# Values of nine of twelve heads turned to tokens by transposing DMA transfers

## The chip, the core and the metric

One core of a Trainium2 chip runs the whole program. Its engines work at the same time, each through its own queue in order: TensorE (PE, with its weight loads PEld), VectorE (DVE), ScalarE (ACT), GpSimd (POOL) and SyncE (SP). SP's queue issues the DMA transfers of the kernel before, and 16 DMA engines carry them out. Waits between engines are semaphores. The metric is the time of one execution on the device in microseconds; lower is better.

## The reference

A trunk of two layers on 528 tokens (16 learned meta tokens ahead of 512 given ones), each of 1024 numbers. Each layer normalises the rows, projects them, mixes the tokens, multiplies with a SiLU gate and projects back. The first is gated linear attention with 4 heads:

```python
S_new = exp(b_last) * S + einsum('bhjd,bhjv->bhdv', k * exp(b_last - b), v)
o = einsum('bhij,bhjv->bhiv', attn, v) + einsum('bhid,bhdv->bhiv', q * exp(b), S)
```

The second is differential attention with 8 heads, the difference of two softmaxes with a shared position bias:

```python
p = softmax(s, axis=-1)
a = p[:, :, 0] - lam * p[:, :, 1]
o = einsum('bhqk,bhkv->bhqv', a, vh)
```

In both, the values v stand on the contracted side: the product over tokens needs them with tokens on the partitions. A head of the first layer has 512 value columns, one of the second 256.

## The kernel before

All matrix products run as three products of rounded parts: a number is split into a high part (fp32r) and a low part, its rest. `split` (line 237) has ACT write the high part (line 240) and DVE the low part (line 241). `split3` (line 328) does the same for 32 short rows that carry the 16 meta tokens, with the parts below each other in one tile (lines 333, 334, 338).

In the projections the weights are the stationary operand, so each result comes out turned: columns of the projection on the partitions, 528 tokens along the row. Most of them are done by halves with seven products in place of eight: a `Unit` (line 362) computes four pieces of a 2 x 2 block product, with sums of weights that DVE makes beforehand (line 296) and partial results that ACT copies out of PSUM (`partial`, line 378). A product is 12 matmuls into one of the banks bx, by and bv. When a piece of 128 columns is complete, the unit calls its `tail(i)`, with i = 1 and then 0.

The weights come by DMA on SP's queue into two buffers named raw (lines 249 and 256). A buffer is free for the next load when DVE's last split has read it.

`Weaver` (line 73) weaves two streams of work into PE's order, which is written out by hand: the attention's own steps, and a queue of projections as generators. `fill(us)` runs that much of the queue, `finish` runs it to a stop mark, and every yielded amount of PE time goes through `spent`, which counts down the steps deferred by `defer`. The order on ACT, DVE, POOL and SP is left to a scheduler; what is marked `urgent` moves forward by 100 places in it.

The values arrive as two pieces a unit. For the first layer, `q_gla_v` (line 755) makes two units a head, so four pieces; each tail calls `turned_back` (line 758), which defers by 2.4 us of PE time a `post`: `to_tokens` (line 730) transposes the piece on PE, four blocks of 128 x 128 (line 735) and one of 128 x 32 for the short rows (line 736), into two PSUM tiles, and `split` and `split3` take them from there into s.v and s.vm. For the second layer `q_diff_v` makes one unit a head, and `turned_back2` (line 1381) does the same with tokens in reversed order. Head 0 of either layer goes its own way (`plain_unit`, and a projection at the layers' boundary), but through the same two functions. This makes 16 + 16 pieces.

`gla_blocks` uses a first-layer head's values when the queue of its projections is finished. In the second layer the step C (`values`, line 1497) uses them, after A (`scores`), B (`turn`: the attention matrix transposed on PE and split into aT and am) and before E (`rows`). For the four blocks b the written order is A3 A2 B3 A1 C3 B2 E3 A0 C2 B1 E2 C1 B0 E1 C0 E0, so B of the next block always stands behind C of the last one.

`b_all` (line 482) holds the first layer's decay sums, one row of 528 for each of 8 column tiles. hT, yt and the others are the residual and intermediate tiles.

Of the kernel before, what the change touches and what calls it, by code (L numbers as in the profile page):

```python
# [11 lines left out]
F32 = mybir.dt.float32  # L12
F32R = mybir.dt.float32r
I32 = mybir.dt.int32
AF = mybir.ActivationFunctionType
ALU = mybir.AluOpType
AX = mybir.AxisListType
# [2 lines left out]
P = 128  # L20
D = 1024
NM = 16
M3 = 96
NR = 512
# [48 lines left out]
class Weaver:  # L73


    def __init__(self):
        self.queue, self.late, self.left, self.stop = deque(), [], 0.0, None

    def add(self, gen, us=0.0):
        self.queue.append(gen)  # L80
# [7 lines left out]
    def defer(self, us, fn):  # L88
        self.late.append([us, fn])

    def spent(self, us):
        for d in self.late:
            d[0] -= us
        while self.late and self.late[0][0] <= 0:
            self.late.pop(0)[1]()
# [33 lines left out]
class Weights:  # L129
# [44 lines left out]
    def done(self, p):  # L174
        self.room[p.kind] += 1
        self.pump()
# [8 lines left out]
def trunk(ctx, tc, x, meta, g_norm, gla_w_in, gla_w_gate_up, gla_b_gate, gla_gnorm, gla_w_out,  # L185
# [3 lines left out]
    act, dve, pe, pool, sp = nc.scalar, nc.vector, nc.tensor, nc.gpsimd, nc.sync  # L189
# [17 lines left out]
    def T(p, shape, dt, tag, **kw):  # L207
        uid[0] += 1
        return p.tile(shape, dt, tag=tag, name=f"{tag}_{uid[0]}", **kw)
# [62 lines left out]
    W = Weaver()  # L272
# [208 lines left out]
    X = {n: x_parts(i) for i, n in enumerate(("b11", "b21", "b22", "t1", "t2", "t4"))}  # L481
    b_all = T(kp, [P, KT, L], F32, "keep")
    hp = ctx.enter_context(tc.tile_pool(name="hp", bufs=1))
    gctx = ctx.enter_context(ExitStack())
    hT = T(hp, [P, KT, L], F32, "hT")
    gp = gctx.enter_context(tc.tile_pool(name="gp", bufs=1))
# [3 lines left out]
    def tmp():  # L490
        return T(tp, [P, L], F32, "t")


    ones = cp.tile([P, P], F32, name="ones")
    dve.memset(ones, 1.0)
# [18 lines left out]
    for b in range(5):  # L514
        t0, n = BLK[b]
# [239 lines left out]
    def q_gla_v(hd, s):  # L755
        us = [want_unit(g_w_in, 2048 + 512 * hd + c) for c in (0, 256)] if hd else v_first

        def turned_back(m, vt):
            def post():
                pt, pm = to_tokens(vt, BLK, vt[:, :32])  # L760
                cs = slice(m * P, (m + 1) * P)
                split(s.v[0][:, :, cs], s.v[1][:, :, cs], pt.rearrange("p (b c) -> p b c", b=4))
                split3(s.vm[:, cs], pm, 32, short[:, NM:NM + 1])
            W.defer(2.4, post)

        gens = []
        for h, u in enumerate(us):
            vts = []

            def dst(h=h, vts=vts):  # L770
                if h == 0:
                    s.vm = T(gp, [M3, 512], F32R, "vm0")
                    s.v = [T(gp, [P, 4, 512], F32R, f"v{i}") for i in range(2)]
                vts.extend([tmp(), tmp()])
                return vts

            if hd:
                gens.append(W.add(Unit(u, X, 1.0, dst, lambda i, h=h, vts=vts: turned_back(2 * h + i, vts[i]))))
            else:
                def evac(i, banks, h=h, vts=vts, dst=dst):  # L780
                    if i == 0:
                        dst()
                    for n, bank in enumerate(banks):
                        act.activation(vts[i][:, n * HT:(n + 1) * HT], bank[:, :HT], AF.Copy)
                    turned_back(2 * h + i, vts[i])

                gens.append(W.add(plain_unit(u, evac)))
        return gens[0]
# [356 lines left out]
    for hd in range(G_HEADS):  # L1145
        s = heads[hd]
        last = hd == G_HEADS - 1
        if hd:
            if not last:
                q_gla_out(hd - 1, heads[hd - 1])  # L1150
            for half in range(2):
                q_gla_z(hd, s, half)
            if not last:
                W.stop = q_gla_qk(hd + 1, heads[hd + 1])[0]
            if hd == 1:
                second_layer_setup()
            W.fill(4.0)
        if hd == 0:
            W.fill(2.0)
        gla_scores(hd, s)  # L1160
        W.fill(5.0)
        gla_ready(hd, s)
        if hd == 0:
            hot = T(gp, [P, TLEN], F32, "kd")
            sp.dma_start(hot[:NBUCK + 1], c_hot)
        W.finish()
        W.settle()
        if hd == 0:
            for m in range(4):
                gla_gate(0, s, m, h2(s.z[:, m, :]))  # L1170
        if hd == 0:
            q_gla_qk(1, heads[1])
        W.stop = None
        if last:
            q_gla_out(hd - 1, heads[hd - 1])
        else:
            W.stop = q_gla_v(hd + 1, heads[hd + 1])
        gla_blocks(hd, s, (1.2, 1.2) if last else (1.9, 1.6), last)
        W.finish()
        W.stop = None  # L1180
# [200 lines left out]
    def turned_back2(s, m, vt, first=False):  # L1381
        if not first:

            urgent(dve.tensor_copy)(vt[:, HT:HT + 8], vt[:, 2 * HT:2 * HT + 8])

        @urgent
        def post():
            end = L if first else 272
            pt, pm = to_tokens(vt, RBLK if first else HBLK, vt[:, end - 32:end])
            cs = slice(m * P, (m + 1) * P)  # L1390
            split3(s.vm[:, cs], pm, 32, short[:, NM + 1:NM + 2])
            split(s.v[0][:, :, cs], s.v[1][:, :, cs], pt.rearrange("p (b c) -> p b c", b=4))
        W.defer(2.2 if s is not heads[-1] else 1.4, post)

    def q_diff_z(hd, s):
        zts = []
# [59 lines left out]
    def diff_steps(hd, s, ys):  # L1456
# [26 lines left out]
        @urgent  # L1483
        def turn(r):
            b, a = r.b, r.p[0]
            pt, pm = ps_tile(), ps_tile()
            for j in range(b + 1):
                pe.transpose(pt[:, j * P:(j + 1) * P], a[:, j * P:(j + 1) * P], ident)  # L1488
            pe.transpose(pm[:32, :P], a[:, r.nk - 32:r.nk], ident)
            r.am = T(ep, [M3, P], F32R, "am")  # L1490
            r.aT = [T(ep, [P, 512], F32R, f"aT{i}") for i in range(2)]
            w = (b + 1) * P
            split(r.aT[0][:, :w], r.aT[1][:, :w], pt[:, :w])
            split3(r.am, pm[:32, :P], 64)
# [129 lines left out]
    for hd in range(D_HEADS):  # L1624
        last = hd == D_HEADS - 1
        s = heads[hd]
        W.finish(projs[hd])
        W.settle()
        s.scored = False
        out2 = None  # L1630
        keep = {D_HEADS - 1: 0.0, D_HEADS - 2: 22.0}.get(hd, 3.0)
        if hd in (2, 4, 6):
            out2 = q_diff_out2(hd - 2, ys[hd - 2:hd])
        if not last:
            n = heads[hd + 1]
            late = hd == D_HEADS - 2
            if not late:
                gates.append(q_diff_z(hd + 1, n))
                values.append(q_diff_v(hd + 1, n))
            W.stop = q_diff_k(hd + 1, n)  # L1640
            projs.append(q_diff_q(hd + 1, n))
            if late:
                values.append(q_diff_v(hd + 1, n))
                gates.append(q_diff_z(hd + 1, n))
        if hd == D_HEADS - 2:
            ws.room["none"] = 0
            wt = want_last(hd)

            def freed():
                ws.room["none"] += 2  # L1650
                ws.pump()
            gates[-1].freed = freed
        (A, B, C, E), o = diff_steps(hd, s, ys), (3, 2, 1, 0)
        steps = [(A, 0), (A, 1), (B, 0), (A, 2), (C, 0), (B, 1), (E, 0), (A, 3), (C, 1), (B, 2), (E, 1), (C, 2), (B, 3),
                 (E, 2), (C, 3), (E, 3)]
        steps = [(f, o[i]) for f, i in steps]
        share = {A: 1.5, B: 1.1, C: 1.1, E: 0.5}
        if last:
            steps = steps[:6]
        W.fill(3.0)  # L1660
        for n, (f, b) in enumerate(steps):
            if last and n == 4:
                if values[hd] in W.queue:
                    W.finish(values[hd])
                W.settle()
                W.fill(2.0)
            if n == 5 and gates[hd] in W.queue:
                W.finish(gates[hd])
            if last and n == 5:
                gfin = T(xp, [P, D], F32, "x0", bufs=1)  # L1670
                sp.dma_start(gfin, g_final.partition_broadcast(P))
            if n == 5:
                if out2 in W.queue:
                    W.finish(out2)
                ys.append([yt[:, hd % 2, i] for i in range(2)])
            f(b)
            if f is A and b == 0:
                s.scored, W.stop = True, None
                if not last:
                    heads[hd + 1].T = bias_tile(hd + 1)  # L1680
            W.fill(max((W.left - keep) * share[f] / sum(share[g] for g, _ in steps[n:]),
                       (4.0 if hd % 2 == 0 else 3.0) if n == len(steps) - 2 else 2.4 if f is C else 0.0))
# [56 lines left out]
```

## Time and profile before

| | |
|---|---|
| median of 3 runs | 996.02 us (995.7 to 997.62) |
| the profiled execution | 998.37 us, its span 996.6 us |
| instructions in the span | 18277 |
| DMA | 84.24 MB, mean 85 GB/s |
| granted TensorE clock, mean | 0.994 |

A row of the groups' view names line, engine, operation, written tile <- read tiles, shapes and count, then the busy time in us and the mean of one in ns, then the idle time of the engine just before them and what ended it. A row of the timeline has its start and its length in us, the engine, the line, the operation and how many were merged; in brackets stands the idle time before it and the releaser. In the table of stretches there follow on the stretch its length, the busy time and count of PE, PEld, DVE, ACT and POOL, the granted clock, DMA's busy share and GB/s. The view of waits names who waited for whom: total us, times, longest. An issue row of DMA gives count, KB of each and the median time from issue to landing. Weight loads and matmuls overlap; some matmul records are missing (120 of 128 on line 735).

### The profile page before, as it was taken

The page shows a single profiled execution, that of the slowest core. Times are in us where ns is not written, and L with a number is a line of the kernel's source. Part 1 is how long each engine was busy: PE and PEld are TensorE (multiplying, and loading weights), DVE is VectorE, ACT ScalarE, POOL GpSimd, SP SyncE. Part 2 cuts the span into 40 slices and gives each one's busy share as a digit, 9 for nine tenths or more (in the row PEclk, how much of TensorE's full clock was granted, in tenths as well). Part 3 has the DMA queues.
Part 4 walks back from the last instruction along what each step waited for, and adds up shares of the span by engine and source line. Part 5 has one row for each costly group of instructions (what it writes and reads, how often), then busy time and mean ns, then how long its engine had stood idle before and what let it go on. Part 6 is the DMA issues. An engine that isn't in the chain of part 4 may idle for free. (4 is left out here: it accounts for less than half of the span.)

```text
span 996.6 us, 18277 instructions
## 1 busy us (share of the span) xinstructions
PE 979.5 (98%) x7143; PEld 925.1 (93%) x7143; DVE 783.2 (79%) x1586; ACT 596.7 (60%) x1304; POOL 48.3 (5%) x68
## 2 busy tenths in 40 slices
PE   8999999999999999999999999999999999999997
PEld 7999999999999999999899898899998999988896
DVE  7888886878777788565998886888967878767785
ACT  7675854365535656536667676366764666645584
POOL 1000000001000100000000100000010010000001
PEclk8999999999999999999999999999999999999999
DMA  7213322132233312222332322333322332323212
GB/s 194 79 50 85 88 84 84 49 108 61 85 85 85 85 47 82 86 85 85 96 86 69 88 68 96 85 97 85 85 96 81 82 103 56 110 62 93 85 65 85
DMA packets 121161, 84.24 MB, mean 85 GB/s; under 512 B 6365, under 2 KB 110077, under 8 KB 121072
## 3 DMA queue, kind: packets, MB, share of 16 engines
q1 hardware_dynamic: 121072, 83.05, 28.8%
q8 instruction: 56, 0.92, 0.4%
q14 instruction: 33, 0.27, 0.1%
HBM read 83.64 MB, written 2.12 MB: 86 GB/s over the span
## 5 line engine op out<-in xcount | busy, mean ns | idle before, releaser
L240 ACT ACTIVATE wh<-raw 128x1024 fp32r<-128x1024 f32 x99 | 104.4, 1055 | 59.6 <-PE by L830 26.9
L241 DVE TENSOR_TENSOR wl<-raw,wh 128x1024 fp32r<-128x1024 f32 x99 | 120.9, 1221 | 24.3 <-ACT wh L240 16.3
L357 PE MATMUL bv<-x,wh 128*128 128x264 f32 (+1 forms) x656 | 97.3, 287 | 0.0
L357 PE MATMUL bx<-x,wh 128*128 128x264 f32 (+1 forms) x640 | 95.2, 286 | 1.0 <-ACT u L378 1.0
L357 PEld LDWEIGHTS bv<-x,wh 128*128 128x128 f32 x656 | 86.3, 189 | 0.3
L357 PEld LDWEIGHTS bx<-x,wh 128*128 128x128 f32 x640 | 84.6, 188 | 2.0 <-ACT u L378 1.5
L241 DVE TENSOR_TENSOR wl<-sum,wh 128x1024 fp32r<-128x1024 f32 x41 | 50.1, 1222 | 21.7 <-ACT wh L240 19.6
L378 ACT ACTIVATE u<-bx 128x264 f32<-128x264 f32 (+1 forms) x120 | 45.4, 379 | 32.4 <-PE bx L357 30.4
L347 PE MATMUL bx<-x,wh 128*128 128x512 f32 (+1 forms) x256 | 62.4, 385 | 0.0
L1475 ACT ACTIVATE p<-p,st 128x528 f32<-128x528 f32 (+3 forms) x64 | 36.4, 569 | 39.2 <-DVE st L1473 39.2
L357 PE MATMUL bv<-x,wl 128*128 128x264 f32 (+1 forms) x328 | 56.4, 286 | 0.0
L357 PE MATMUL bx<-x,wl 128*128 128x264 f32 (+1 forms) x320 | 54.6, 285 | 0.0
L240 ACT ACTIVATE wh<-sum 128x1024 fp32r<-128x1024 f32 x41 | 43.3, 1055 | 18.2 <-PE by L830 9.6
L347 PEld LDWEIGHTS bx<-x,wh 128*128 128x128 f32 x256 | 44.5, 188 | 7.9
L1511 POOL TENSOR_TENSOR st<-st,mhalf 128x1 f32<-128x1 f32 x32 | 28.1, 879 | 474.3 <-ACT on L1509 426.3
L357 PE MATMUL by<-x,a12h 128*128 128x264 f32 (+1 forms) x320 | 46.5, 285 | 0.0
L357 PEld LDWEIGHTS bv<-x,wl 128*128 128x128 f32 x328 | 46.2, 189 | 0.1
L357 PE MATMUL bx<-x,a11h 128*128 128x264 f32 (+1 forms) x320 | 46.2, 285 | 0.0
L240 ACT ACTIVATE a11h<-raw 128x512 fp32r<-128x512 f32 x41 | 25.8, 628 | 33.2 <-DMA raw<-in_diff_w_in_dram 17.6
L357 PEld LDWEIGHTS bx<-x,wl 128*128 128x128 f32 x320 | 45.3, 188 | 0.1
L357 PEld LDWEIGHTS bx<-x,a11h 128*128 128x128 f32 x320 | 42.3, 189 | 0.8
L357 PEld LDWEIGHTS by<-x,a12h 128*128 128x128 f32 x320 | 41.7, 188 | 0.0
(465 smaller groups left out, 2652.4 us busy)
## 6 DMA issues: line engine op xcount, KB each, us to landing
raw<-in_gla_w_in_dram SPq DMA_DIRECT2D x48, 512.0 KB, 4.2
raw<-in_diff_w_in_dram SPq DMA_DIRECT2D x42, 512.0 KB, 5.6
raw<-in_diff_w_in_dram SPq DMA_DIRECT2D x11, 1024.0 KB, 5.8
raw<-in_gla_w_out_dram SPq DMA_DIRECT2D x8, 1024.0 KB
raw<-in_diff_w_out_dram SPq DMA_DIRECT2D x8, 1024.0 KB, 5.0
T<-bdr SPq DMA_DIRECT2D x8, 264.0 KB
out_dram<-x SPq DMA_DIRECT2D x8, 256.0 KB, 2.1
kd<-steep SPq DMA_DIRECT2D x4, 400.0 KB
```

The costliest lines, as they stand in the source:

```text
L240: act.activation(hi, src, AF.Copy)
L241: dve.tensor_tensor(lo, src, hi.bitcast(F32), op=ALU.subtract)
L347: pe.matmul(bank, a[:, k, :], b[k] if n0 is None else b[k][:, n0 + i * nn:n0 + (i + 1) * nn], start=n == 0 and ks[0] == 0, stop=n == len(t ...
L357: pe.matmul(bank[:, :x[q].shape[2]], w[p][:, k * P:(k + 1) * P], x[q][:, k, :], start=first and i == 0, stop=i == len(PASSES) - 1, skip_gr ...
L378: act.activation(t, self.bx[:, :self.n], AF.Copy, scale=self.sc)
L1475: act.activation(p[:, :nk], p[:, :nk], AF.Exp, scale=-1.0, bias=st[:, m:m + 1], accum_out=st[:, 2 + m:3 + m])
L1511: pool.tensor_tensor(ms, ms, mhalf[:, :1], op=ALU.pow)
```

## The change

For heads 1 to 3 of the first layer and heads 1 to 6 of the second, `to_tokens` is no longer called. In its place `turn_by_dma` handles a pair of pieces:

- `leave(m, src)`, called by a unit's tail: ACT copies the piece into a plane, as 16-bit words, all low halves of the 32-bit numbers first and all high halves behind them; ACT then issues a DMA that writes the plane to DRAM (vd, three buffers).
- When both pieces have left, `follow` puts two steps on the weaver's list: `turn` after 6.0 us of PE time, and `done` another 9.0 us later.
- `turn`: SP issues transposing DMAs of 16-bit words from vd back into the planes' own bytes (one of four blocks in the first layer, two of two blocks in the second, where the slices reverse the order of the blocks), and one more for the short rows into a tile `lands`. Rows of vd are ordered piece, partition, half; so the two halves of a number land next to each other, and both pieces of the pair side by side.
- `done`: `split` and `split3` read from the landed tiles, once for the pair, 256 columns wide.

The planes of the first layer lie in rows of b_all whose decays have been read; those of the second are a new tile with one buffer. For its room aT and am have one buffer where they had two. `land` empties the list: before a head's `gla_blocks`, and at the start of a head of the second layer.

```diff
 class Weaver:
+        self.away = []
...
+    def follow(self, *steps):
+        self.away.append([steps[0][0], list(steps)])
+
+    def onward(self, us=0.0):
+        for d in list(self.away):
+            d[0] -= us
+            while d[0] <= 0:
+                d[1].pop(0)[1]()
+                if not d[1]:
+                    self.away.remove(d)
+                    break
+                d[0] += d[1][0][0]
+
+    def land(self):
+        while self.away:
+            self.onward(1000.0)
+
     def spent(self, us):
+        self.onward(us)
...
+    def words(t):
+        return t.bitcast(U16)
+
+    def turn_by_dma(planes, groups, ends, done):
+        n = planes.shape[2]
+        vd = T(dp, [2, P, 2, n], U16, "vd", bufs=3)
+        rows = vd.rearrange("m p h c -> (m p h) c")
+        raw = planes.rearrange("p m c -> p (m c)")[:, :2 * NR].rearrange("p (b c) -> p b c", c=2 * P)
+        left, lands = [0, 1], []
+
+        @urgent
+        def leave(m, src):
+            pl = words(planes[:, m, :]).rearrange("p (h c) -> p h c", h=2)
+            act.activation(pl, words(src).rearrange("p (c h) -> p h c", h=2), AF.Copy)
+            act.dma_start(vd[m], pl)
+            left.remove(m)
+            if not left:
+                W.follow((6.0, turn), (9.0, lambda: done(raw, lands[0][:32, 0, :])))
+
+        def turn():
+            for blocks, c0 in groups:
+                o = words(raw[:, blocks, :])
+                sp.dma_start(o, rows[:, c0:c0 + P * o.shape[1]], transpose=True)
+            lands.append(T(mp, [P, 1, 2 * P], F32, "lands"))
+            sp.dma_start(words(lands[0]), rows[:, ends:ends + P], transpose=True)
+
+        return leave
...
+        def turner(h):
+            @urgent
+            def done(pt, pm):
+                cs = slice(256 * h, 256 * h + 256)
+                split(s.v[0][:, :, cs], s.v[1][:, :, cs], pt)
+                split3(s.vm[:, cs], pm, 32, short[:, NM:NM + 1])
+            return turn_by_dma(b_all[:, 2 * h:2 * h + 2, :], [(slice(0, 4), NM)], 0, done)
...
-                gens.append(W.add(Unit(u, X, 1.0, dst, lambda i, h=h, vts=vts: turned_back(2 * h + i, vts[i]))))
+                gens.append(W.add(Unit(u, X, 1.0, dst, lambda i, vts=vts, leave=turner(h): leave(i, vts[i]))))
...
+        W.land()
         gla_blocks(hd, s, (1.2, 1.2) if last else (1.9, 1.6), last)
...
-        W.defer(2.2 if s is not heads[-1] else 1.4, post)
+        @urgent
+        def done(pt, pm):
+            split3(s.vm, pm, 32, short[:, NM + 1:NM + 2])
+            split(s.v[0], s.v[1], pt)
+
+        if first or s is heads[-1]:
+            W.defer(2.2 if first else 1.4, post)
+        else:
+            if m:
+                s.leave = turn_by_dma(T(ep, [P, 2, 536], F32, "planes", bufs=1),
+                                      [(slice(3, 1, -1), 0), (slice(1, None, -1), 272)], 240, done)
+            s.leave(m, vt[:, :536])
...
-            r.am = T(ep, [M3, P], F32R, "am")
-            r.aT = [T(ep, [P, 512], F32R, f"aT{i}") for i in range(2)]
+            r.am = T(ep, [M3, P], F32R, "am", bufs=1)
+            r.aT = [T(ep, [P, 512], F32R, f"aT{i}", bufs=1) for i in range(2)]
...
         W.settle()
+        W.land()
         s.scored = False
```

More of the change, by code (lines that the diff above doesn't have):

```diff
@@ L14 @@
 I32 = mybir.dt.int32
+U16 = mybir.dt.uint16
 AF = mybir.ActivationFunctionType
@@ L483, in trunk @@
     hp = ctx.enter_context(tc.tile_pool(name="hp", bufs=1))
+    mp = ctx.enter_context(tc.tile_pool(name="mp", bufs=1))
     gctx = ctx.enter_context(ExitStack())
```

## The prediction

> **What bounds the kernel now.** I read the page's first part, then the stretches of the span, then PE's own view around one of the groups that the change removes.
>
> ```profile
> span 996.6 us, 18277 instructions
> ...
> PE 979.5 (98%) x7143; PEld 925.1 (93%) x7143; DVE 783.2 (79%) x1586; ACT 596.7 (60%) x1304; POOL 48.3 (5%) x68
> ...
> PEclk8999999999999999999999999999999999999999
> ...
> q1 hardware_dynamic: 121072, 83.05, 28.8%
> ```
> ```profile
> 146.00:250.00 104.00, 103.52 (x817) 100.12 (x816) 79.81 (x152) 54.71 (x107) 3.57 (x5) 1.00 0.29 82
> 250.00:355.00 105.00, 104.69 (x833) 102.37 (x833) 81.97 (x153) 57.31 (x111) 3.57 (x5) 1.00 0.28 81
> ...
> 530.00:910.00 380.00, 379.32 (x2607) 351.26 (x2606) 299.19 (x653) 231.09 (x556) 23.37 (x25) 1.00 0.29 85
> ```
>
> The columns of the second fence are stretch, length, then PE, PEld, DVE, ACT and POOL busy, the granted clock and DMA's share. The stretches hold two heads of the first layer and the second layer's heads. PE is idle for 0.3 to 0.7 us in each, at full clock; ACT has 40% to 47% of them free and DVE some 22%. So every slot that leaves PE shortens the span, as long as no other engine makes PE wait; and there is almost no waiting on PE now that could absorb a new one. DMA has 70% of its time free.
>
> **PE: what is removed.** Each of 24 calls of to_tokens loses four transposes of 128x128 and one of 32 columns (lines 735 and 736).
>
> ```profile
> 726.59 0.47 PEld L735 LDWEIGHTS ps<-ident,t 128*128 128x128 f32 x4
> ...
> 727.02 0.10 PEld L736 LDWEIGHTS ps<-ident,t 128*32 128x32 f32 x1
> ...
> 727.13 0.42 PEld L357 LDWEIGHTS bx<-x,wl 128*128 128x128 f32 x3
> ...
> 729.17 1.32 PE L326 MATMUL ps<-v,aT 128*128 128x256 f32 x9
> ```
> ```profile
> L735 PE MATMUL ps<-ident,t x120: 270/272/282, 38.2 to 953.8; 128*128 128x128 f32 x120
> ```
>
> The first weight load of the group starts at 726.59, the first of the product behind it at 727.13: a group holds PE for 0.54 us. 24 x 0.54 = **13.0 us off PE**. A rival that they stay does not arise: in the order of the built program the 120 transposes of tiles t are 24. The Trainium skill, "TensorE: Matmul & The Clock Gate", Part 4, gives about 275 ns for a 128x128 transpose within a kernel. The last row agrees as to the duration (272 ns), but they overlap on PE; five times 275 ns would make an estimate of 33 us for 24 groups, and the starts say 13.0.
>
> **ACT and DVE: what is added and taken away.** For each pair of pieces (12 of them), ACT makes two plane copies of 128x1056 or 128x1072 words (line 532 of the changed kernel), issues two DMAs, and then splits one 128x1024 tile where it split two of 128x512.
>
> ```profile
> L240 ACT ACTIVATE wh<-raw 128x1024 fp32r<-128x1024 f32 x99 | 104.4, 1055 | 59.6 <-PE by L830 26.9 <-PE bv L357 11.1 <-PE bx L347 9.7
> ...
> L240 ACT ACTIVATE v<-ps 128x512 fp32r<-128x512 f32 x32 | 19.0, 595 | 5.9 <-PE ps L735 5.4
> ...
> L334 ACT ACTIVATE vm<-ps,short 32x128 fp32r<-32x128 f32 x32 | 11.3, 357 | 0.5
> ...
> L333 ACT ACTIVATE vm<-ps,short 32x128 fp32r<-32x128 f32 x32 | 10.9, 343 | 0.0
> ```
> ```profile
> 598.05 0.37 SPq L249 DMA_DIRECT2D raw<-in_diff_w_out_dram  x1
> ```
>
> A plane copy by the elements of the 1024-wide row: 1.055 x 1056/1024 = 1.09 us. A DMA's issue by SP's: 0.37. Added: 2 x (1.09 + 0.37) = 2.9 us a pair. Taken away: two splits of 0.595 for one of 1.055 (0.1), and four short ones of 0.34 to 0.36 for two of twice the width, some 0.4 each (0.6). Net 2.2 us a pair, 26 us over 12: ACT goes from 597 to 623 us, still under two thirds. DVE only gets less. As totals both lie beside PE. What counts is the bunch: ACT reads each partial product (line 378) out of bank bx before PE may go on in it, and PE has one product in another bank meanwhile:
>
> ```profile
> 937.02 1.14 PE L357 MATMUL by<-x,a12h 128*128 128x264 f32 x8
> ...
> 938.48 1.14 PE L357 MATMUL bx<-x,wh 128*128 128x264 f32 x8
> ```
>
> One product is 938.48 - 937.02 = 1.46 us, so a bunch on ACT beyond about 1.5 us reaches PE. In the built order both copies and both issues stand back to back in 4 of the 12 pairs, and in a fifth with one weight split between; I count 5: 5 x (2.9 - 1.46) = 7.2; in the other 7 other work stands between, which I price at nothing because 1.46 us of product covers each half. Bounds: 0 (all hidden) to 12 x 1.44 = 17. I take **+7**.
>
> **The new wait.** ACT's split of the landed values waits for a chain: second DMA out, SP's wake-up, transpose in. What stands behind it on ACT are the partial products, the weight splits and the scores' exponentials, and behind those PE. How much time the order leaves for the chain is read from the trace of before at the same neighbours. The first pair's second issue stands behind the copy u of the first row below, and its split behind the cm of the second row; the last pair's between the third and fourth.
>
> ```profile
> 158.25 0.39 ACT L378 ACTIVATE u<-bx 128x264 f32<-128x264 f32 x1 [0.87 <-PE bx L357]
> ...
> 166.41 0.27 ACT L334 ACTIVATE cm<-ps 32x128 fp32r<-32x128 f32 x1
> ```
> ```profile
> 856.61 0.36 ACT L378 ACTIVATE u<-bx 128x264 f32<-128x264 f32 x1
> ...
> 862.13 0.27 ACT L334 ACTIVATE am<-ps 32x128 fp32r<-32x128 f32 x1
> ```
>
> From end to end that is 8.0 us and 5.4 us. Taken so for the 12 pairs (2.9 us off where the bunch stands inside) it lies between 4.7 and 8.4, 6.9 on average. The chain:
>
> ```profile
> raw<-in_gla_w_in_dram SPq DMA_DIRECT2D x48, 512.0 KB, 4.2
> raw<-in_diff_w_in_dram SPq DMA_DIRECT2D x42, 512.0 KB, 5.6
> ...
> out_dram<-x SPq DMA_DIRECT2D x8, 256.0 KB, 2.1
> ```
>
> - Out: 264 to 268 KB like the output's 256 KB, 2.1 us; the second, right behind the first or beside a weight load, at most twice that. I take 3.0.
> - SP: one issue, 0.4.
> - In: 512 KB are transposed, and 128 KB more for the short rows. No row shows a transposing DMA. The nearest is a weight piece of 512 KB: 4.2 us from issue to landing. The short rows add between nothing and a quarter of that (1.05); I take 0.7, since they run on behind the first. Together 4.9.
>
> Sum 8.3, against 6.9: 1.4 us for each pair, on an ACT whose wait goes straight on to PE because the splits behind it come at once. 12 x 1.4 = **+17**. Bounds from the rows: with the transfer at 2.1 us, the fastest of its size class, the chain is 2.1 + 0.4 + 2.1 = 4.6 and nothing is left to wait for: 0, and less than no wait there is not. From above, each partition receives 16-bit words of many rows; the built transfer moves blocks of 16 rows, thus pieces of 32 bytes, 16384 of them for 512 KB. What a tiny piece costs shows where single words were loaded:
>
> ```profile
> DMA packets 1689, 0.01 MB, mean 5 GB/s; under 512 B 1689, under 2 KB 1689, under 8 KB 1689
> ...
> q1 hardware_dynamic: 1689, 0.01, 64.2%
> ```
>
> This is the stretch from 21.8 to 23.2: 0.642 x 16 engines x 1.4 us / 1689 = 8.5 ns each. 16384 / 16 x 8.5 ns = 8.7 us, a quarter more for the short rows 10.9: chain 3.0 + 0.4 + 10.9 = 14.3, wait 7.4 a pair, 89 in all. I stay with the weight piece: it has the size, the queue and the direction of these transfers, and its 4.2 us lies between the two ends.
>
> **At nothing.** aT and am with one buffer: PE runs values(b) before turn(b+1) in the written order, so the next transposes already stand behind the last read; without that cover each turn would wait for one group of values, up to the 1.3 us of the row at 729.17, 32 times. DMA's load: 12 x (0.54 out + 0.66 in) = 14 MB beside 83, a share of 34% after 28.8%. The planes and lands with one buffer each are written again a head or 10 us of work later.
>
> **Sum.** -13.0 + 7 + 17 = **+11 us**. Against the profiled execution that is a span of 996.6 + 11 = 1007.6; that execution took 998.4, the median of the runs 996.0, so I add to the median: **1007 us**, 1.1% slower.
>
> **Rivals.**
> - *The transposes run at copying speed and land in time* (chain of 4.6 to 6.5 against 6.9). Then only the bunches remain: -13 + 7 = -6, 990 us. For it: 70% of DMA's time is free, and the output's 256 KB need only 2.1 us. Against: two pairs leave 5.4 us or less, and a weight piece on the same queue needs 4.2 on its own. The Trainium skill speaks for this case: "Advanced Engine Details and Errata", X-Bar Transpose (TRN2), has transposes as fast as ordinary DMAs, and "DMA: Bandwidth & Descriptors", Latency and other measured facts, gives 261 GB/s for a kernel's transposes, an estimate of 2.0 us for 512 KB. The Trainium skill's table in the first of these, DGE: Hardware vs Software, speaks against the change: it rates transposes through hardware queues, such as SP's, as less efficient than through software. No row here shows either.
> - *The pieces of 32 bytes decide* (slower side, from some 3 us more per transfer on): -13 + 7 + 89, 1079 us. For it: the 8.5 ns row; against: a transposing path would be of no use at that price.
> - *SP's queue*: the transposes wait on SP for the data to land, and weight loads stand behind them. In before the load at 598.05 goes out beside the second layer's bias; in the changed order it and its like in two later heads stand behind a pair's transposes, some 5 us later (3.0 out, 0.4, three more issues of 0.4 and the bias load). ACT waits for raw in places already:
>
> ```profile
> ACT a11h L240 <- DMA raw<-in_diff_w_in_dram: 17.6, 5, 5.1
> ```
> ```profile
> SPq L256 <- DVE wl L241: 381.8, 34, 20.2
> ```
>
> If all three are needed at once, 3 x 5 = 15 on top of the forecast: 1022 us. Against: loads wait on SP for a free buffer, 381.8 / 34 = 11 us each, which hides most of it.
> - *The two sides cancel*: the wait at a third of my price, -13 + 7 + 6: 996 us.
>
> **Chances.** Forecast 0.49 (its own range 999 to 1030), copying speed 0.27, pieces 0.11, SP's queue 0.06, cancelling 0.07. Under 0.2% (2 us) a measurement cannot tell a difference from none. Faster 0.27, same 0.07, slower 0.66. The range from 986 to 1045 leaves out most of the pieces' case and the lower end of the copying one.
>
> **What would show it.** Right: line 735 with 24 transposes, PE busy some 13 us less, a longer span; ACT's splits of v and vm waiting for DMA by 1 to 2 us a pair; PE idle where the bank bx is read late. The out transfers landing in 2 to 3 us and the transposes in 4 to 5. Wrong: transposes landing in under 3 us and no wait of ACT on them (990), or in 8 and more (over 1050); or the weight splits waiting for raw in place of v.

## The result, and the profile after

The changed kernel takes **1030.72 us** (median of 4 runs, 1028.51 to 1031.73) against 996.82 us of the kernel before on the same chip (4 runs, 995.7 to 998.57). The ratio is 1.0335 with a 95% interval of 1.0311 to 1.0359: 3.4% slower. The forecast was 1007 us; the sign and the outer range (986 to 1045) were right, but the time lies 0.7 us above the forecast's own range (999 to 1030), and the loss is 34 us where 11 were expected.

The page of the changed kernel, its span, busy times and DMA queues:

```profile
span 1029.9 us, 18079 instructions
...
PE 983.0 (95%) x7023; PEld 922.1 (90%) x7023; DVE 778.1 (76%) x1562; ACT 613.3 (60%) x1292; POOL 48.2 (5%) x68
...
q1 hardware_dynamic: 152752, 90.92, 32.8%
q10 hardware_dynamic: 3456, 6.54, 1.8%
```

Two things are to be seen. PE lost 120 instructions, the transposes, and yet its busy time rose by 3.5 us. And the part of the span in which PE is not busy rose from 996.6 - 979.5 = 17.1 us to 1029.9 - 983.0 = 46.9, by 29.8.

The view of waits says who waited (total us, times, longest):

```profile
DVE v L263 <- ACT v L262: 33.1, 11, 6.0
...
ACT v L262 <- DMA planes<-vd: 25.3, 6, 6.8
...
ACT a11h L262 <- DMA raw<-in_diff_w_in_dram: 19.3, 6, 4.9
...
PEld ps L1592 <- ACT on L1586: 14.2, 6, 4.7
ACT v L262 <- DMA keep<-vd: 13.5, 6, 3.8
...
PE ps L1592 <- ACT on L1586: 11.6, 6, 4.2
...
ACT a11h L262 <- DMA raw<-in_gla_w_in_dram: 10.2, 5, 4.9
```

ACT waits for the landed values at all twelve pairs, 25.3 + 13.5 = 38.8 us (keep is b_all, the planes of the first layer), and DVE behind it. PE's own loss in the second layer stands at line 1592, the transposes of step E (line 1518 before): they wait for `on`, which ACT normalises. ACT's wait for weight pieces (raw) is nearly as before in the second layer (17.6 us there) and longer in the first (6.5 us there). SP waits as well: in its own view it stands 41.9 us for outs to land before it can issue the transposes.

```profile
SPq L541 <- DMA vd<-planes: 29.5, 6, 6.6
...
SPq L541 <- DMA vd<-keep: 12.4, 5, 6.8
```

One pair in the timeline, the second layer's fourth changed head: ACT, SP and PE.

```profile
749.45 0.34 ACTq L533 DMA_DIRECT2D vd<-planes  x1
...
754.25 0.27 ACT L356 ACTIVATE am<-ps 32x128 fp32r<-32x128 f32 x1
761.31 1.06 ACT L262 ACTIVATE v<-planes 128x1024 fp32r<-128x1024 f32 x1 [6.80 <-DMA planes<-vd]
...
766.25 0.46 ACT L1586 ACTIVATE on<-ps,st 128x256 f32<-128x256 f32 x1
```
```profile
755.90 2.58 SPq L541 DMA_TRANSPOSE planes<-vd  x2
758.53 1.26 SPq L543 DMA_TRANSPOSE lands<-vd  x1
```
```profile
766.77 0.69 PE L1592 MATMUL ps<-ident,on 128*128 128x128 f32 x2 [4.22 <-ACT on L1586]
```

The second out is issued at 749.45, SP begins the transposes 6.45 us later, and ACT's split starts 5.4 us after that. ACT has had nothing to do since 754.52. The normalisation `on`, written behind the split, is therefore done only at 766.71, and PE stands still for 4.22 us. What follows the stall is seen in the table of stretches (stretch, length, busy time and count of PE, PEld, DVE, ACT, POOL, granted clock, DMA share, GB/s):

```profile
758.00:762.50 4.50, 4.50 (x22) 3.34 (x20) 0.10 (x1) 1.19 (x2) 0.00 (x0) 1.00 0.61 113
762.50:766.70 4.20, 0.05 (x1) 0.00 (x0) 3.91 (x7) 4.15 (x13) 0.55 (x1) 1.00 0.00 0
766.70:770.08 3.38, 3.31 (x11) 2.93 (x12) 2.31 (x7) 2.47 (x8) 0.00 (x0) 0.50 0.46 157
770.10:790.00 19.90, 19.90 (x95) 16.54 (x95) 12.86 (x27) 7.58 (x16) 0.55 (x1) 1.00 0.26 80
```

Right behind the stall PE works for one stretch at half clock: 11 matmuls in 3.4 us. The records of the granted clock hold seven such stretches of 3.41 us in this execution, each at 2.0 to 4.2 us in which PE stood still, in one to three pieces; the kernel before has none in this part of the span (26 to 990 us). They cost up to 7 x 3.41 x 0.5 = 11.9 us, and since a matmul at half clock counts as busy, they hide in PE's busy time.

So the 33.3 us between the spans are 29.8 of PE standing still, 11.9 of half clock and -13.0 of transposes; the 4.6 left are in the lengths of PE's records, whose ends are modelled, and aren't resolved.

The times of the new transfers, from the DMA issues (count, KB, median us from issue to landing) and from the view of the tile vd (min/median/max ns that the issue takes on SP's queue):

```profile
raw<-in_gla_w_in_dram SPq DMA_DIRECT2D x48, 512.0 KB, 5.3
...
vd<-planes ACTq DMA_DIRECT2D x12, 268.0 KB, 3.0
vd<-keep ACTq DMA_DIRECT2D x12, 264.0 KB, 2.2
...
planes<-vd SPq DMA_TRANSPOSE x12, 4.1
keep<-vd SPq DMA_TRANSPOSE x6, 6.6
```
```profile
L543 SPq DMA_TRANSPOSE lands<-vd x12: 1237/1254/2422, 164.9 to 891.4; - x12
...
L541 SPq DMA_TRANSPOSE planes<-vd x12: 1235/1288/1422, 560.6 to 890.0; - x12
L541 SPq DMA_TRANSPOSE keep<-vd x6: 1961/3468/4295, 161.0 to 398.3; - x6
```

Few landings can be timed: the 6.6 us is one transfer, the 4.1 the middle of two. ACT waited for all six transfers of 512 KB (keep), so its start shows when they had landed: 4.2 to 7.8 us after the issue. The seven weight pieces of 512 KB in the first row that can be timed took 3.9 to 8.6 us.

### The profile page after: what moved, and what is told of

It is laid out like the page before. It is cut to its first block, busy times and chain, and to the rows that moved or that the text cites. A ratio compares the mean times of both kernels' runs of the same rounds, so it can differ in the third digit from the quotient of the medians.

```text
span 1029.9 us, 18079 instructions
## 1 busy us (share of the span) xinstructions
PE 983.0 (95%) x7023; PEld 922.1 (90%) x7023; DVE 778.1 (76%) x1562; ACT 613.3 (60%) x1292; POOL 48.2 (5%) x68
## 3 DMA queue, kind: packets, MB, share of 16 engines
q1 hardware_dynamic: 152752, 90.92, 32.8%
## 5 line engine op out<-in xcount | busy, mean ns | idle before, releaser
L379 PEld LDWEIGHTS bx<-x,wh 128*128 128x128 f32 x640 | 85.4, 190 | 5.8 <-ACT u L400 5.0
L369 PE MATMUL bx<-x,wh 128*128 128x512 f32 (+1 forms) x256 | 64.5, 395 | 2.6 <-ACT ps L1582 1.6
L263 DVE TENSOR_TENSOR wl<-sum,wh 128x1024 fp32r<-128x1024 f32 x41 | 50.1, 1222 | 21.0 <-ACT wh L262 19.6
L262 ACT ACTIVATE wh<-sum 128x1024 fp32r<-128x1024 f32 x41 | 43.2, 1054 | 25.3 <-PE by L891 8.6
L369 PEld LDWEIGHTS bx<-x,wh 128*128 128x128 f32 x256 | 46.0, 195 | 11.6 <-ACT ps L1582 2.1
```

The source lines that it names most:

```text
L262: act.activation(hi, src, AF.Copy)
L263: dve.tensor_tensor(lo, src, hi.bitcast(F32), op=ALU.subtract)
L369: pe.matmul(bank, a[:, k, :], b[k] if n0 is None else b[k][:, n0 + i * nn:n0 + (i + 1) * nn], start=n == 0 and ks[0] == 0, stop=n == len(t ...
L379: pe.matmul(bank[:, :x[q].shape[2]], w[p][:, k * P:(k + 1) * P], x[q][:, k, :], start=first and i == 0, stop=i == len(PASSES) - 1, skip_gr ...
```

## Experiments

Theory 1: the loss is ACT's wait for the landed values. The scheduler puts the splits into ACT's and DVE's queues at a place where the transposes haven't landed; what stands behind them, PE's partial products and the normalisations, comes late, and PE's stalls bring half clock on top. Rival 2: the added work costs by itself (2a the bunches on ACT, 2b the transfers and SP's queue). Rivals 3 and 4 are on the distance: 15 us too short, or the written 9 us too short. A rival to the scheduler's part in theory 1 is the mark `urgent` on `done`, which moves it forward as well; no run takes that mark alone away.

In the table, idle is the span less PE's busy time, and half clock is the sum of the stretches at a granted clock of 0.5 between 30 and 985 us. Each ratio is to the runs of the kernel before that were made with that run; their medians are 996.8 to 998.6 us.

| run | median us | ratio to before (95%) | span | PE busy | idle | half clock |
|---|---|---|---|---|---|---|
| before | 996.82 | | 996.6 | 979.5 | 17.1 | 0 |
| after | 1030.72 | 1.0335 (1.0311 to 1.0359) | 1029.9 | 983.0 | 46.9 | 23.9 |
| all on PE, copies | 1001.57 | 1.0039 (1.0025 to 1.0052) | 998.2 | 977.9 | 20.3 | 0 |
| ... and outs | 1010.95 | 1.0144 (1.0120 to 1.0168) | 1006.1 | 980.2 | 25.9 | 0 |
| ... and transposes | 1015.19 | 1.0173 (1.0156 to 1.0190) | 1012.7 | 982.6 | 30.1 | 3.4 |
| pinned, 9 us behind the out | 1013.68 | 1.0159 (1.0140 to 1.0179) | 1011.6 | 976.2 | 35.4 | 17.1 |
| pinned, 15 us | 997.96 | 0.9983 (0.9968 to 0.9999) | 998.6 | 971.3 | 27.3 | 3.4 |
| pinned, 26 us | 1003.66 | 1.0053 (1.0032 to 1.0073) | 1002.0 | 970.9 | 31.1 | 10.2 |
| 26 us written, not pinned | 1030.06 (one run) | | 1028.3 | 980.2 | 48.1 | 23.9 |
| first layer alone, pinned | 991.18 | 0.9928 (0.9914 to 0.9942) | 990.4 | 972.2 | 18.2 | 0 |
| all nine heads, pinned | 993.72 | 0.9961 (0.9946 to 0.9976) | 992.5 | 968.2 | 24.3 | 3.4 |
| eight heads, pinned | 993.57 | 0.9949 (0.9930 to 0.9968) | 989.5 | 968.1 | 21.4 | 0 |

### All that is added, but nothing waits for it

```diff
-                W.follow((6.0, turn), (9.0, lambda: done(raw, lands[0][:32, 0, :])))
+                W.follow((6.0, turn))
...
-                gens.append(W.add(Unit(u, X, 1.0, dst, lambda i, vts=vts, leave=turner(h): leave(i, vts[i]))))
+                gens.append(W.add(Unit(u, X, 1.0, dst, lambda i, h=h, vts=vts, leave=turner(h): (leave(i, vts[i]), turned_back(2 * h + i, vts[i])))))
```

and the same in `turned_back2`.

> All nine heads' values are turned on PE as in the kernel before, and what the change adds on the way is issued as well: plane copies and out DMAs on ACT, the transposing DMAs on SP, one buffer for aT and am. The landed tiles are not read, so nothing waits for them. Theory 1 (the time went into ACT's wait for the landed tiles, which PE catches at full and which costs the clock on top): without that wait the bunches on ACT and SP's longer issues are nearly hidden, 997 to 1006 us, no stall of PE over 2 us in a changed head and no stretch of half clock. Rival 2 (the bunches of copies and issues on ACT, SP's holding and DMA's load cost by themselves): 1015 us and more, since after is 1030.7 and PE is given back 13 us of transposes.

Measured: 1015.19 us, 1.73% above before, PE's idle time up by 13 us, one stretch of half clock. Rival 2's number came out, and theory 1's 997 to 1006 us did not: the added work costs some 17 us here even if nothing reads its result. But the run isn't the changed kernel less its wait: it keeps the 24 groups of transposes and their 48 small splits and adds the copies beside them, so ACT is fuller (619.4 us busy) than in the changed kernel (613.3). What it settles is that the second term isn't zero, and that without ACT's wait the half clock all but goes.

### The splits pinned to their written place

```diff
-    def split(hi, lo, src, scale=None):
+    def split(hi, lo, src, scale=None, pin=lambda i: i):
...
-            act.activation(hi, src, AF.Copy)
-            dve.tensor_tensor(lo, src, hi.bitcast(F32), op=ALU.subtract)
+            pin(act.activation(hi, src, AF.Copy))
+            pin(dve.tensor_tensor(lo, src, hi.bitcast(F32), op=ALU.subtract))
...
-                split(s.v[0][:, :, cs], s.v[1][:, :, cs], pt)
+                split(s.v[0][:, :, cs], s.v[1][:, :, cs], pt, pin=tc.keep_in_program_order)
```

and likewise `split3` and the second layer's `done`.

> The changed kernel; only the instructions of done (ACT's and DVE's splits of the landed values) now keep the place in their engines' queues at which they are written, 15 us of PE time behind the second out, where before the scheduler moved them forward. Theory 1: the wait of ACT and DVE on planes and keep goes from 38.7 us to under 8, the stretches of half clock go, and of the 34 us between 996 and 1030 more than 30 come back: 985 to 1000 us. Rival 2 (bunches, SP, DMA): nothing of those is touched, 1020 to 1031 us. Rival 3 (15 us is still too short since the transposes land that late): 1005 to 1020, with the waits at half.

Measured: 997.96 us. No transfer, no copy, no byte is different from the changed kernel, and PE, SP and POOL have their instructions in the same order in both traces. On ACT and DVE the five pinned instructions a pair have moved: the split of v stands 2 to 26 places later on ACT in eleven pairs of the twelve. The scheduler also moved some others past neighbours, about 20 of ACT's other 1280 and 40 of DVE's other 1538, mostly weight splits. The whole loss of 33 us comes back: between the two traces PE's idle time differs by 19.6 us and the half clock by 20.5 us, which is worth some 10.2, of 31.3 us between the spans. Of the wait for landed values the view of waits has one entry left:

```profile
ACT v L262 <- DMA keep<-vd: 1.4, 1, 1.4
```

Theory 1's number came out, and rival 3's did not: the place of the splits is what the loss hangs on. What remains open is why the kernel isn't faster than before although PE has 13 us less to do.

### The same, later

```diff
-                W.follow((6.0, turn), (9.0, lambda: done(raw, lands[0][:32, 0, :])))
+                W.follow((6.0, turn), (20.0, lambda: done(raw, lands[0][:32, 0, :])))
```

> As the run with the pinned splits, with 26 us of PE time between the second out and the splits in place of 15. Theory 1: the transposes have long landed by then, so the same time as with 15 us to within 4 us, or a few us more where the splits now stand close ahead of the products that read them. Rival 3 (15 us too short): clearly faster than with 15, by 5 us and more.

Measured: 1003.66 us, 6 us more than with 15; rival 3 falls here too. By the path at equal places of PE's order the first layer was 5.9 us ahead of the kernel before until its last head; then one stall took it all. PE's timeline:

```profile
406.76 0.58 PE L1141 MATMUL ps<-vm,am 96*16 96x512 f32 x1 [7.82 <-ACT vm L356]
```

The last head's splits, written that late, stand directly ahead of the products that read them. So the right distance is not one number: heads 1 and 2 have room for 26 us, head 3 has not.

### Only the written delay

The same edit on the changed kernel, without the pin.

> The changed kernel with one number changed: done follows 20 us of PE time behind the transposes in place of 9; nothing is pinned. Theory 1 (the scheduler puts the splits where its own reckoning has the transposes landed, whatever the written place): the same order on ACT, 1026 to 1034 us, waits of ACT on planes and keep still 30 to 40 us. Rival 4 (the written delay of 9 us was simply chosen too short): the waits go and the time falls below 1005 us.

Measured: 1030.06 us in one run, waits on planes and keep 27.4 + 15.6 = 43.0 us, somewhat above the range, and six half-clock stretches (23.9 us). Rival 4 falls: all twelve splits of v stand at the same places of ACT's order as with 9 us, so a number that is written in the code and looks like the distance has no say here. Whether the scheduler's own reckoning of the landing or the mark `urgent` puts them there isn't shown.

```profile
ACT v L262 <- DMA planes<-vd: 27.4, 6, 7.0
...
ACT v L262 <- DMA keep<-vd: 15.6, 6, 4.0
```

### The added work in steps

First the copies alone, then the copies and outs, on the kernel of the first experiment:

```diff
-            act.dma_start(vd[m], pl)
...
-                W.follow((6.0, turn))
+                pass
```

> All values turned on PE; of the change only ACT's 24 plane copies and the single buffers of aT and am are added, no out DMA, no transposing DMA. Measured so far: with copies, outs and transposes, but no wait for them, +17 us. Theory 2a (ACT's bunches of copies make up these 17 us): +10 us and more here, 1008 and up. Theory 2b (the 17 us come from the transfers: weight pieces that land later beside them, and SP held by the transposes' issue): 0 to +3 us here, 997 to 1001 us. The prediction's own term (7 us for the bunches, issues included) would be +3 to +5.

> As the run with the copies alone, and ACT issues the 24 out DMAs as well; no transposes. It splits the rest of the 17 us. If SP's issue of the transposes decides (each pair holds SP 3.9 us in the second layer and weight loads stand behind it): 998 to 1005 us, and the rest up to 1015 comes with the transposes. If ACT's DMA issues or the out transfers beside the weight loads decide: 1008 us and more.

Measured: 1001.57 and 1010.95 us. The copies and the single buffers together cost 3.5 us in the medians (between 2a and 2b, and what the prediction's term had for copies), the outs 9.4 more, the transposes 4.2 more; the last step isn't clear of the noise, since the two intervals overlap in the table. So the outs are the largest part, ahead of SP's issues, against my first guess. The run doesn't separate the transfers from ACT's 24 issues of 0.34 us. Of the 7.9 us between the spans without and with outs, 4.7 are two places (2.2 and 2.5 us) where PE stands behind a DVE that waits for weight pieces. One of them on DVE, with outs and before:

```profile
685.89 0.69 DVE L318 TENSOR_TENSOR sum<-raw 128x512 f32<-128x512 f32 x1 [3.16 <-DMA raw<-in_diff_w_in_dram]
```
```profile
678.75 1.23 DVE L241 TENSOR_TENSOR wl<-raw,wh 128x1024 fp32r<-128x1024 f32 x1 [0.67 <-ACT wh L240]
...
681.98 0.69 DVE L296 TENSOR_TENSOR sum<-raw 128x512 f32<-128x512 f32 x1 [0.30 <-DMA raw<-in_diff_w_in_dram]
```

With the outs the two weight pieces have landed 7.3 us after the first one's issue (678.61 on SP's queue), before 5.9 us (676.12); and DVE's order now has the sum, which waits for them, ahead of the split `wl`, which was ahead of it before. PE waited 2.2 us there. Such a place belongs to this order of instructions: with all heads pinned it is not there.

### The first layer alone

Heads 1 and 2 pinned 26 us behind the out, head 3 15 us; the second layer as before, its aT with two buffers again. `turn_by_dma` takes the two times as an argument.

```diff
-            return turn_by_dma(b_all[:, 2 * h:2 * h + 2, :], [(slice(0, 4), NM)], 0, done)
+            return turn_by_dma(b_all[:, 2 * h:2 * h + 2, :], [(slice(0, 4), NM)], 0, done, ((6.0, 20.0), (6.0, 20.0), (6.0, 9.0))[hd - 1])
...
-        if first or s is heads[-1]:
-            W.defer(2.2 if first else 1.4, post)
+        if True:
+            W.defer(2.2 if s is not heads[-1] else 1.4, post)
```

> Only the three heads of the first layer go by DMA, with the splits pinned 26 us of PE time behind the second out for heads 1 and 2 and 15 us for head 3; the second layer is as before. The runs with 15 and 26 us showed the path 1.9 us shorter by the end of head 3 with 15, and 5.9 us shorter until just ahead of head 3's products with 26, where 8.1 us were then lost to a wait for the splits. Theory 1 (the price is where the splits stand): the 6.5 us of PE time of 12 groups come through nearly whole, 989 to 993 us, faster than both kernels. If the two placements do not add up: 994 to 998.

Measured: 991.18 us, ratio 0.9928 (0.9914 to 0.9942): faster than both kernels, and in theory 1's range. Twelve groups at 0.54 us are 6.5 us, and 998.05 - 991.18 = 6.9 came through. The page:

```profile
span 990.4 us, 18174 instructions
...
PE 972.2 (98%) x7083; PEld 918.3 (93%) x7083; DVE 780.0 (79%) x1574; ACT 605.2 (61%) x1298; POOL 47.3 (5%) x68
```

PE's idle time is 18.2 us, 1.1 more than before, and its busy time 7.3 us less. The view of waits has no wait for landed values left, and the transposing transfers are hidden as a whole.

### All nine heads, and all but one

```diff
-                                      [(slice(3, 1, -1), 0), (slice(1, None, -1), 272)], 240, done)
+                                      [(slice(3, 1, -1), 0), (slice(1, None, -1), 272)], 240, done, (6.0, 20.0))
```

> As the run with the first layer's heads alone, and the six heads of the second layer go by DMA too, with their splits pinned 26 us behind the second out. Theory 1 with the second layer's price from the run with 26 us (from +2.2 at head 1's products of PE to +5.4 at the end, thus +3): 992 to 997 us. If the second layer's relief of 6.5 us came through as the first's does: 984 to 987 us.

Measured: 993.72 us, within theory 1's numbers. The second layer gives 2.5 us away where it has 6.5 to win. About half of those 9.0 us is lost in its first changed head: at equal places of PE's order, the run leads the kernel before by 7.2 us just before a stall there and by 2.6 us just after it. SP, ACT and PE there:

```profile
542.69 2.59 SPq L541 DMA_TRANSPOSE planes<-vd  x2
545.34 1.26 SPq L543 DMA_TRANSPOSE lands<-vd  x1
546.70 9.11 SPq L278 DMA_DIRECT2D raw<-in_diff_w_in_dram  x4
```
```profile
550.93 0.63 ACT L262 ACTIVATE a11h<-raw 128x512 fp32r<-128x512 f32 x1 [5.50 <-DMA raw<-in_diff_w_in_dram]
```
```profile
557.00 0.44 PE L1592 MATMUL ps<-ident,on 128*128 128x128 f32 x2 [3.23 <-ACT on L1586]
```

SP issues in order: from 538.5 it waits 4.1 us for the second out to land, then three transposes hold it for 4.0 us, and the weight pieces go out behind them, 8.5 us after the bias load that stands ahead (T, 538.20); in the kernel before it is 0.4 us (545.04 and 545.42). ACT waits 5.5 us for the first piece, the normalisation stands behind that, and PE stalls by 3.2 us with a stretch of half clock to follow. So I left this head to PE:

```diff
-        if first or s is heads[-1]:
-            W.defer(2.2 if first else 1.4, post)
+        if first or s in (heads[1], heads[-1]):
+            W.defer(2.2 if s is not heads[-1] else 1.4, post)
```

> As the run with all nine heads pinned (993.7 us), but head 1 of the second layer is turned on PE as before. In that run SP issued head 1's three transposes from 542.7 to 546.7 us and four weight pieces behind them; ACT waited 5.5 us for the first of these, PE 3.2 us at step E, and 3.4 us at half clock followed. Theory 1 with the SP queue as the rest of the price: these 3.2 + 1.7 us and some 1.5 us of smaller stalls behind them go, 1.1 us of relief is given up: 988 to 991 us. If what is lost in the second layer lies elsewhere (the single buffers, the copies): 993 to 995 us.

Measured: 993.57 us (987.99 to 995.05), outside the 988 to 991 of theory 1 and within the 993 to 995 of the other reading. In the profiled execution (991.26 us) the stall and the half clock of this head are gone and the span is 3.0 us shorter than with all nine; but the runs of this kernel spread over 7 us, and the two intervals overlap. That SP's queue causes the stall is read from the rows; that its removal is worth 3 us isn't shown by the medians.

### A shorter distance, pinned

```diff
-                W.follow((6.0, turn), (9.0, lambda: done(raw, lands[0][:32, 0, :])))
+                W.follow((6.0, turn), (3.0, lambda: done(raw, lands[0][:32, 0, :])))
```

> The splits pinned 9 us of PE time behind the second out, where the runs with 15 us (998.0) and 26 us (1003.7) did not wait for the landed tiles. Theory 1: the chain of out, SP's issue and transposes takes 9 to 12 us, so ACT waits 1 to 3 us for most pairs, 15 to 30 us in all on planes and keep, and the stalls and half clocks come back in part: 1005 to 1022 us. If the pin itself, and not the distance, was what helped: 996 to 1001 us with no wait on planes and keep over 1 us.

Measured: 1013.68 us, in theory 1's range, so the pin alone isn't what helped. The way there was another than I wrote: the wait on planes and keep is only 4.5 us, not 15 to 30. The first layer has two stalls of PE of 2.2 and 2.6 us behind it, with half clock; in the second layer the splits, 2.1 us of ACT in a row, stand ahead of the aT that PE needs, and ACT waits 6.7 us for a weight piece behind SP's transposes:

```profile
551.67 2.59 SPq L541 DMA_TRANSPOSE planes<-vd  x2
...
555.67 10.13 SPq L278 DMA_DIRECT2D raw<-in_diff_w_in_dram  x4
```
```profile
566.99 0.44 PE L1592 MATMUL ps<-ident,on 128*128 128x128 f32 x2 [4.41 <-ACT on L1586]
```

This last stall has its like with 15 us (4.0 us at 562.2), so it isn't what sets the two runs apart; of the 13.0 us between their spans, PE's idle time makes 8.1 and half clock some 6.8, all over the program. So a place costs more than the wait for the data that it makes: the two waits are 4.5 and 1.4 us, and the times are some 16 us apart.

## Why the prediction was wrong in size

**PE, -13.0 us: right.** 24 groups of five transposes are gone; where the stalls are few, PE's busy time fell by 11.3 us (all nine heads pinned) and 7.3 us (the first layer, 6.5 expected).

**The bunches, +7 us: near as a size, by luck, and wrong as a cause.** With all nine heads pinned, everything but the wait cost 993.7 - (998.05 - 13.0) = 8.7 us; with all of them at 15 us it is 998.0 - (998.6 - 13.0) = 12.4, so the size hangs on the places. A copy took 1.08 us (said 1.09), an issue 0.34 (0.37), but two copies and two issues back to back took 2.44 us and not 2.9, as an issue runs beside the next copy. The copies with the single buffers cost some 3.5 us (2.5 to 5.2 by the interval). The rest came with the outs and the transposes: weight pieces that land later and go out behind SP's transposes are seen in the rows above, and the share of ACT's issues stays open.

**The new wait, +17 us: this step failed.** ACT waited 38.8 us for the landed values where the sum had 17, and the pin took back 33 us. (The pin changes the places as well as the wait, so the 33 us aren't the wait alone.) Three parts of the term were off:

- The chain. From the second out's issue to the start of the split it took 6.4 to 11.9 us, 9.5 on average over the twelve pairs, where I had 8.3. The way to SP's start was right on average only (3.5, said 3.0 + 0.4): it is 2.2 to 3.6 us in eight pairs and 4.9 to 6.5 in four of the second layer. The way in took 6.0 in place of 4.9: SP itself is held by a transposing issue, 1.2 to 1.4 us for 256 KB and 2.0 to 4.3 for 512 KB where I wrote 0.4, and from the issue of 512 KB to ACT's start it took 4.2 to 7.8 us, where I had the weight piece's 4.2 and 0.7 for the short rows.
- The window. 9.5 less ACT's wait of 38.8 / 12 = 3.2 leaves 6.2 us, where I had read 6.9 from the neighbours in the kernel before. Chain and window together make 3.2 us a pair in place of 1.4.
- What a stall costs. I priced a us of ACT's wait as a us of PE. Against the pinned kernel PE stood still for only 19.6 us more, about half of ACT's wait. But behind a stall of 2 to 4 us the granted clock was 0.5 for a stretch: up to 11.9 us in this execution that no term of my sum held. The two errors work against each other.

**The place.** I expected PE to stand where bank bx is read late. It stands at step E in the second layer (line 1592, 11.6 us of the view of waits), since the normalisation is behind the split on ACT, and in the first layer at products into bv, which DVE frees late: at 185.3 PE stands for 3.7 us behind DVE's line 899, after DVE has waited 2.5 us for ACT's vm of the landed values. That vm was late in its turn because ACT had waited 1.9 us for a weight piece (until 182.76), so not all of this stall is the wait for the values.

**At nothing.** DMA's load was 32.8 + 1.8 = 34.6% (said 34). The single aT and am cost, with the copies, some 3.5 us. The planes' and lands' buffers were no one's wait in the changed kernel; with all nine heads pinned, SP waits 8.2 us in three places of the first layer for a buffer of lands.

**The rivals.** *Copying speed* fell: the transposes land in 4.1 and 6.6 us, not in 2.1, and the chain is 9.5 us where this rival had 4.6 to 6.5. The Trainium skill's "Advanced Engine Details and Errata", X-Bar Transpose (TRN2), has them as fast as ordinary DMAs. Here 512 KB took 4.2 to 7.8 us against 3.9 to 8.6 for a weight piece on the same queue, which shows no difference; 256 KB took 4.0 and 4.2 us against 2.0 to 3.5 for ordinary transfers of about that size the other way. *Pieces of 32 bytes* fell from the other side: 14.3 us of chain against 9.5. The pieces were larger too: queue q1 moved 31680 packets and 7.87 MB more than before, about 250 bytes a packet. *SP's queue*, which I gave 6 in 100, is there. Weight loads stand behind SP's 41.9 us of waiting for the outs and behind the transposes, and ACT's waits for raw sum to 33.2 us (25.4 before). In the changed kernel that stays below the wait for the values; it shows once that wait is gone (second layer with 15 us, pinned: 26.7 us, before 17.6). That *the two sides cancel* is the pinned kernel with 15 us, by chance.

## What to carry to other kernels

An instruction that waits for a DMA chain belongs in an in-order queue at a place where the chain has landed on the chip, but not directly ahead of its reader. Where a scheduler builds the queue, look up the place in the built order, and fix it if need be; here the same work is 3.4% slower or 0.4% faster by the places, and a written delay that didn't change the order looked like a remedy and was none. Price a stall of PE not by its length alone, but with the half clock that follows it. And count a transposing DMA as holding its issuing queue for microseconds, first while its source lands and then for its issue (here 4.1 and 4.0 us in one head): what else is on that queue, weight loads above all, comes later.

## What the runs showed of the hardware

- **Half clock after short stalls.** In the nine traces in which PE stalled by 2 us or more in one piece, all 13 stalls of 2.6 us or more were followed by a stretch at a granted clock of 0.5 (from 0.6 us ahead of their end to 1.2 us behind it; once it began within a stall of 7.8 us). Of nine between 2.0 and 2.6 us, four were; single stalls below 2.0 us never, and shorter ones close together sometimes. A stretch lasts 3.41 us, three times 6.83; at half clock 3.41 us are worth some 1.7, so by this estimate such a stall costs 1.7 us more than its length. The Trainium skill, "TensorE: Matmul & The Clock Gate", Part 1, puts the gate at one idle window of some 3.4 us. Here 2.6 us were enough each time.
- **A transposing DMA holds SP.** In the changed kernel its issue takes 1.24 to 1.42 us for 256 KB, about the same (median 1.25, up to 2.4) for the short rows' 128 KB, 2.0 to 4.3 us for 512 KB, beside 0.34 us for an out's issue on ACT and a median of 0.37 for the other issues on SP.
